# The head of a decoder trunk: where the first modulation sums are computed, and in which order its tiles are split

## The chip, the cores and the metric

One core of a Trainium2 chip runs the kernel. The metric is device microseconds of a whole execution. Three runs of the kernel before gave 1766.54, 1766.80 and 1773.45, median 1766.8. The profiled execution took 1766.12, its span is 1764.3.

## The reference

One layer on 2048 tokens of width 1024. The change lies in the first line's `shift` and `scale` and in the first projections.

```python
mod = jax.nn.silu(c) @ w_ada[l] + b_ada[l]
shift, scale, gate = jnp.split(mod, 3, axis=-1)
u = x * (1.0 + scale[:, None, :]) + shift[:, None, :]
h = u @ w_in[l]
q, k, v, a_gate, p_in, p_gate, m_a, m_p = jnp.split(h, offsets, axis=-1)
a = sliding_window_sink_attention(q, k, v, sinks[l], bias, mask) * jax.nn.silu(a_gate)
...
y = (y @ w_out[l]) * (1.0 + gate[:, None, :])
x = layer_norm(DEEPNORM_ALPHA * x + y, ln_gain[l], ln_bias[l])
```

## The kernel before

**Numbers.** A f32 value is held as a high part (a cast to a shorter f32 form, done on ACT) and a low part (value minus high part, done on DVE). A product of two such values is three TensorE products: high by high, high by low, low by high (`mm3`). I call these three a triple.

**Products.** The projections use a Strassen-like scheme with seven products instead of eight. A group of the work has two quads; a quad is two weight tiles of 128 columns of `w_in`, and each works on the sets named B11, T1, T2, B21, T3, B22 and T4. A set holds the high and low parts of one quarter of the transposed `u`, or of a sum or difference of quarters, in four tiles of 128 rows by 512 tokens. For each quad the weights are needed in three pairs (`first`, `second`, `third`) and one last half. A pair is split into parts by `pair_split`: a cast on ACT and a subtraction on DVE, each of 128x1024. `sum1`, `mid` and `late` make the sums of the weight quarters.

**The order.** PE, ACT, DVE, POOL and SP each run their own queue in order. Most operations of the head go through a helper that keeps program order, so all have one line in the profile, L56. In the rings after the head, work is hung on places of a group (a position counts ticks, one about every twelve products), and `steps` spreads a list of work over the places from a start on.

**The head** (`head`) opens the program. It computes shift and scale for the eight 128-row tiles k = 0 to 7, modulates the first half of the tokens, builds the sets and begins the first group.

- `load(k)`, on SP: two weight tiles of `w_ada` of 512 KB each, one for shift (`wadat`, laid out for TensorE) and one for scale (`wada`, laid out with the outputs on partitions), and 512 KB of `x`. After tiles 0 and 1 come the four weight quarters of a quad of the first group, 1 MB.
- `opening(k)`: `pe_modulation` multiplies the shift weights, as the stationary side, with single columns of silu(c), in 8 f32 products of 128x1. `modulation` computes scale on DVE as a product and sum over 1024 elements (CUSTOM_DVE_ANT_0 in the profile), and then adds PE's column to shift.
- `difference(k)` on DVE, for k below 4: the T1 difference before modulation. `modulate_x(k)` on ACT: both halves of the tile, in place.
- `middle(k)`: the parts of B11 (k below 4) or B21, one after the other; for k from 4 the raw T2 sum. `closing(k)`: the parts of T1 or T2, two tiles behind.
- `products(i)`: the triples of tile i for B11 and T1 and both quads, three tiles behind `opening`. `second_pair(x)` and `more` make the second pair of a quad and the triples of T2 and B21.
- `rest_sums(i)`: the sums for T3 and T4. Then the parts of T3, and in `first_phase` those of B22 and T4 at positions 4 and 6 of the first group. The same function spreads the second half's work (`sums_to`) from places 4, 29, 57 and 80 on.

The ring (`ring`, `back`) then adds the copies to the products (L380, L383), splits the third pair (L132 for its low part), and runs T3, B22 and T4 for each quad and B11 and T1 for the next group.

Of the kernel before, what the change touches and what calls it, by code (L numbers as in the profile page):

```python
# [12 lines left out]
F32 = mybir.dt.float32  # L13
# [6 lines left out]
P = 128  # L20
# [39 lines left out]
def kernel(  # L60
# [215 lines left out]
    class Quad:  # L276
# [7 lines left out]
        def load(self, ph, own, q=nc.sync, e=nc.gpsimd):  # L284
# [4 lines left out]
            q.dma_start(x[:, 0::3, :], by_two(self.srcs[0]))  # L289
# [824 lines left out]
    def head(ph):  # L1114
# [6 lines left out]
        early = [pl.tile([P, 4 * D], F32, tag=f"set_{n}", name=f"head_{n}") for n, pl in (("B22", cp), ("T3", ph.t), ("T4", ph.t))]  # L1121
        places = [t[:, i * D : (i + 1) * D] for t in (*early, big) for i in range(4)]
        ws = [places[2 * k : 2 * k + 2] for k in range(KT)]
        late = [small[:, i * D : (i + 1) * D] for i in range(2)]
# [15 lines left out]
        def load(k):  # L1140
            for w, m in zip(ws[k], (k, KT + k)):
                sp.dma_start(w, (wadat if m < KT else wada)[m])
# [12 lines left out]
        def pe_modulation(k):  # L1155
            sums[k] = bank(("pv", "pt", "lg", "lg")[k % 4])
            for i in range(KT):
                mm(sums[k][:, 0:1], ws[k][0][:, i * P : (i + 1) * P], ct[:, i : i + 1], start=i == 0, stop=i == KT - 1)

        def modulation(k):  # L1160
            m = KT + k
            w = ws[k][1]
            dve.tensor_tensor_reduce(w, w, cb, 1.0, mod[:, m : m + 1], ALU.mult, ALU.add, mod[:, m : m + 1])
            dve.tensor_tensor(mod[:, k : k + 1], mod[:, k : k + 1], sums[k][:, 0:1], ALU.add)
# [11 lines left out]
        def opening(k):  # L1176
            pe_modulation(k)
            modulation(k)

        def middle(k):  # L1180

            b1, b2 = xs[k]
            if k < 4:
                pool.dma_start(b12_d[k // 2, :, k % 2, :], b2)
            else:
                dve.scalar_tensor_tensor(ts[k - 4], ts[k - 4], sg[:, k - 4 : k - 3], b2, ALU.mult, ALU.add)
            parts("B11" if k < 4 else "B21", k % 4, b1)

# [5 lines left out]
        def closing(k):  # L1194
            if k >= 4:
                parts("T2", k - 4, ts[k - 4])
                return
            hi, lo = sets["T1"][:, k, 0, :], sets["T1"][:, k, 1, :]
            scale = mod[:, KT + k : KT + k + 1]
# [4 lines left out]
        def rest_sums(i):  # L1204
            minus(xs[i][0], ts[i], xs[i][0])
            minus(xs[4 + i][0], xs[4 + i][0], ts[i])
# [276 lines left out]
```

## Time and profile before

| what | value |
|---|---|
| median of 3 runs | 1766.8 us |
| profiled execution | 1766.12 us |
| its span | 1764.3 us |
| PE busy | 1702.9 us, 97% |
| DVE busy | 1206.0 us, 68% |
| ACT busy | 931.8 us, 53% |
| first 512-wide product on PE | 29.93 us |
| last product of T2 and B21 in the head | 64.8 us |

PE counts as busy whenever a product is under way, so its share says nothing on how fast it goes. A timeline row gives start, duration, engine, line, operation, output, input and count, then in brackets the idle time ahead of it and what ended it. Rows that follow each other closely overlap a little: the distance of two starts is the price, the duration has the pipeline's tail in it.

### The profile page before, as it was taken

The page shows a single profiled execution, that of the slowest core. Times are in us where ns is not written, and L with a number is a line of the kernel's source. Part 1 is how long each engine was busy: PE and PEld are TensorE (multiplying, and loading weights), DVE is VectorE, ACT ScalarE, POOL GpSimd, SP SyncE. Part 2 cuts the span into 40 slices and gives each one's busy share as a digit, 9 for nine tenths or more (in the row PEclk, how much of TensorE's full clock was granted, in tenths as well). Part 3 has the DMA queues.
Part 4 walks back from the last instruction along what each step waited for, and adds up shares of the span by engine and source line. Part 5 has one row for each costly group of instructions (what it writes and reads, how often), then busy time and mean ns, then how long its engine had stood idle before and what let it go on. Part 6 is the DMA issues. An engine that isn't in the chain of part 4 may idle for free. (4 is left out here: it accounts for less than half of the span.)

```text
span 1764.3 us, 24983 instructions
## 1 busy us (share of the span) xinstructions
PE 1702.9 (97%) x8248; PEld 1428.7 (81%) x8248; DVE 1206.0 (68%) x2180; ACT 931.8 (53%) x1969; POOL 792.7 (45%) x618
## 2 busy tenths in 40 slices
PE   6899999999999998999999999999999989999996
PEld 5688888888888887888788888888888768888785
DVE  5967665655777786766655367777867586765777
ACT  4544444545777775454444377777744333423451
POOL 2145454431356567434434125456762562364542
PEclk9999999999999999999999999999999999999998
DMA  9384767743354567687777634544796585689432
GB/s 365 112 279 179 270 210 273 271 148 132 108 173 146 172 219 294 245 281 254 246 274 262 231 98 132 175 155 149 258 356 225 182 257 182 226 314 384 166 143 99
DMA packets 180609, 381.30 MB, mean 216 GB/s; under 512 B 18800, under 2 KB 39296, under 8 KB 180480
## 3 DMA queue, kind: packets, MB, share of 16 engines
q1 hardware_dynamic: 173696, 363.66, 59.2%
q0 software_dynamic: 3552, 11.56, 1.7%
q10 hardware_dynamic: 3232, 4.49, 0.9%
q8 instruction: 65, 1.06, 0.2%
q14 instruction: 64, 0.52, 0.1%
HBM read 244.35 MB, written 138.44 MB: 217 GB/s over the span
## 5 line engine op out<-in xcount | busy, mean ns | idle before, releaser
L56 PE MATMUL mm<-set_B,w_set 128*128 128x512 f32 x3240 | 801.8, 396 | 17.5 <-DVE w_set L132 8.7
L56 PEld LDWEIGHTS mm<-set_B,w_set 128*128 128x128 f32 x3240 | 604.2, 189 | 147.4 <-DVE w_set L132 15.2
L56 PE MATMUL lg<-set_T,w_set 128*128 128x512 f32 x2088 | 505.9, 392 | 14.0 <-DVE w_set L132 8.6
L56 PEld LDWEIGHTS lg<-set_T,w_set 128*128 128x128 f32 x2088 | 390.8, 188 | 103.7 <-DVE w_set L132 14.0
L132 DVE TENSOR_TENSOR w_set<-W,w_set 128x1024 fp32r<-128x1024 f32 x162 | 224.1, 1383 | 175.7 <-ACT w_set L325 171.4
L325 ACT CAST w_set<-W 128x1024 fp32r<-128x1024 f32 x162 | 169.7, 1049 | 242.4 <-PE mm L56 195.6
L56 PE MATMUL mm<-set_T,w_set 128*128 128x512 f32 x1080 | 266.2, 394 | 0.0
L56 PEld LDWEIGHTS mm<-set_T,w_set 128*128 128x128 f32 x1080 | 201.1, 189 | 41.3
L294 POOL TENSOR_TENSOR W<-W,A 128x512 f32<-128x512 f32 x56 | 82.1, 1466 | 221.7 <-DMA W<-in_win_dram 55.9
L303 POOL TENSOR_TENSOR W<-W 128x512 f32<-128x512 f32 x56 | 80.1, 1431 | 155.5 <-DVE w_set L132 143.9
L56 DVE TENSOR_TENSOR o<-pv,o 64x128 f32<-64x128 f32 x256 | 72.4, 283 | 88.3 <-ACT o L56 85.4
L56 ACT ACTIVATE L<-L,nm 128x257 f32<-128x257 f32 (+1 forms) x256 | 127.2, 498 | 9.3 <-DVE nm L56 3.9
L298 POOL TENSOR_TENSOR W<-W 128x512 f32<-128x512 f32 x56 | 88.1, 1574 | 93.8 <-DVE w_set L132 84.7
L56 DVE CUSTOM_DVE_ANT_0 L<-lg,bt,nsink 128x256 f32<-128x256 f32 (+1 forms) x256 | 111.6, 473 | 5.0 <-PE lg L56 0.8
L299 POOL TENSOR_TENSOR W<-W 128x512 f32<-128x512 f32 x56 | 88.1, 1573 | 37.3 <-DMA W<-in_win_dram 28.1
L56 POOL TENSOR_TENSOR w_set<-W,w_set 128x1024 fp32r<-128x1024 f32 x14 | 33.7, 2405 | 139.6 <-ACT w_set L56 97.0
L56 POOL TENSOR_TENSOR p<-nxt,pg 128x512 f32<-128x512 f32 x32 | 42.0, 1311 | 106.4 <-DVE sm L56 102.8
L56 ACT COPY o<-pv 64x256 f32<-64x256 f32 x128 | 47.3, 370 | 78.1 <-PE pv L56 77.3
L56 DVE TENSOR_TENSOR ptl<-pt,pth 128x512 fp32r<-128x512 f32 (+1 forms) x128 | 85.7, 669 | 1.9 <-ACT pth L56 1.7
L56 DVE TENSOR_TENSOR k_lo<-spare,k_hi 128x512 fp32r<-128x512 f32 x61 | 63.2, 1041 | 28.8 <-ACT k_hi L56 15.0
L56 PE MATMUL lg<-kk,qs 128*128 128x256 f32 (+1 forms) x512 | 80.5, 279 | 0.0
L56 ACT ACTIVATE L<-L,sm 128x256 f32<-128x256 f32 (+1 forms) x128 | 64.3, 502 | 29.4 <-DVE sm L56 29.4
(208 smaller groups left out, 2304.9 us busy)
## 6 DMA issues: line engine op xcount, KB each, us to landing
W<-in_win_dram SPq DMA_DIRECT2D x48, 512.0 KB, 5.3
w_set<-wmix_d SPq DMA_DIRECT2D x32, 512.0 KB, 5.2
W<-in_win_dram SPq DMA_DIRECT2D x34, 256.0 KB, 3.4
A<-in_win_dram SPq DMA_DIRECT2D x34, 256.0 KB, 5.0
ag_d<-sig SPq DMA_DIRECT2D x32, 256.0 KB, 3.3
pg_d<-sig SPq DMA_DIRECT2D x32, 256.0 KB, 3.7
ma_d<-sig SPq DMA_DIRECT2D x32, 256.0 KB, 3.9
mp_d<-sig SPq DMA_DIRECT2D x32, 256.0 KB, 3.8
```

Of the source, the lines that this page charges most:

```text
L56: return lambda *args, **kw: self.tc.keep_in_program_order(op(*args, **kw))
L132: engine.tensor_tensor(dst, src, as32(hi), ALU.subtract)
L294: e.tensor_tensor(self.w[:, 1, :], self.w[:, 2, :], self.a22, ALU.add)
L298: e.tensor_tensor(x[:, 1, :], x[:, 1, :], x[:, 0, :], ALU.subtract)
L299: e.tensor_tensor(x[:, 2, :], x[:, 0, :], x[:, 2, :], ALU.subtract)
L303: e.tensor_tensor(x[:, 3, :], x[:, 3, :], x[:, 1, :], ALU.subtract)
L325: a.copy(by_two(hi), raw)
```

## The change

All of it is in the head, the load of a quad, and some places of the first ring.

- The modulation weights are the moving side: `pe_rows(k)` multiplies one column of silu(c) as the stationary side with 128 columns of weights, 8 f32 products for a row of 128 results on one partition. ACT copies the row to SBUF, and `pe_columns(k)` turns it to a column with a one-element product.
- For tiles 0 to 3 TensorE computes both rows, shift and scale. The scale weights of these tiles come in TensorE's layout, and DVE's sum over 1024 elements goes. For tiles 4 to 7 scale stays on DVE.
- `keep_going(n)` puts n products of the 128x128 identity with itself on PE: 18 ahead of the first row, 8 behind the first columns.
- `high(k)` makes the high parts of a tile on ACT, `rest_of(k)` the low parts on DVE one tile later. T2 is likewise cut into `raw_t2`, `high_t2` and `low_t2`. `difference(k)` stands ahead of the sum.
- The first pair of each quad is split one by one, behind tiles 0 and 1, instead of both behind tile 2. The products of tile k-2 stand one quad ahead of the row of tile k and one quad behind it. The second pairs stand in the turns k = 6 and 7.
- One weight quarter of each quad is loaded later, behind tiles 4 and 5.
- The sums for T3 stand at the end of the head, each ahead of its parts; those for T4 move to position 5 of the first ring, the late weight sum of the second quad to position 0, and the second half's work starts at 6 and 30 in place of 4 and 29.
- The tiles in which weights wait are taken in another order (T4, T3, B22).

```diff
-        def load(self, ph, own, q=nc.sync, e=nc.gpsimd):
+        def load(self, ph, own, q=nc.sync, e=nc.gpsimd, a12=True):
...
-            q.dma_start(x[:, 0::3, :], by_two(self.srcs[0]))
+            if a12:
+                q.dma_start(x[:, 0::3, :], by_two(self.srcs[0]))
+            else:
+                q.dma_start(x[:, 0, :], self.srcs[0][:, 0:CH])
...
-                sp.dma_start(w, (wadat if m < KT else wada)[m])
+                sp.dma_start(w, (wadat if m < KT or k < 4 else wada)[m])
...
-        def pe_modulation(k):
-            sums[k] = bank(("pv", "pt", "lg", "lg")[k % 4])
-            for i in range(KT):
-                mm(sums[k][:, 0:1], ws[k][0][:, i * P : (i + 1) * P], ct[:, i : i + 1], start=i == 0, stop=i == KT - 1)
+        def rows_of(k):
+            return 2 if k < 4 else 1
+
+        def pe_rows(k):
+            sums[k] = bank(("pv", "pt")[k % 2])
+            for r in range(rows_of(k)):
+                for i in range(KT):
+                    mm(
+                        sums[k][0:1, r * P : (r + 1) * P],
+                        ct[:, i : i + 1],
+                        ws[k][r][:, i * P : (i + 1) * P],
+                        start=i == 0,
+                        stop=i == KT - 1,
+                    )
+            n = rows_of(k) * P
+            act.copy(row_of(k)[:, 0:n], sums[k][0:1, 0:n])
+
+        def pe_columns(k):
+            for r in range(rows_of(k)):
+                mm(sums[k][:, 2 * P + r : 2 * P + r + 1], row_of(k)[:, r * P : (r + 1) * P], one, start=True, stop=True)
...
+        def high(k):
+            if k < 4:
+                pool.dma_start(b12_d[k // 2, :, k % 2, :], xs[k][1])
+            act.copy(part("B11" if k < 4 else "B21", k % 4, 0), xs[k][0])
+            if k < 4:
+                scale = mod[:, KT + k : KT + k + 1]
+                act.activation(part("T1", k, 0), ts[k], AF.Copy, scale=scale)
+                act.activation(sg[:, k : k + 1], scale, AF.Copy, scale=-1.0)
+
+        def rest_of(k):
+            name = "B11" if k < 4 else "B21"
+            low(dve, part(name, k % 4, 1), xs[k][0], part(name, k % 4, 0))
+            if k < 4:
+                scale = mod[:, KT + k : KT + k + 1]
+                dve.scalar_tensor_tensor(part("T1", k, 1), ts[k], scale, as32(part("T1", k, 0)), ALU.mult, ALU.subtract)
...
+        def keep_going(n):
+            acc = bank("lg")
+            for i in range(n):
+                mm(acc[:, 0:P], ident, ident, start=True, stop=True)
+
+        keep_going(18)
+        pe_rows(0)
+        pe_columns(0)
+        keep_going(8)
         difference(0)
+        modulation(0)
         modulate_x(0)
-        opening(1)
+        high(0)
+        first_pair(0)
+        pe_rows(1)
+        pe_columns(1)
         difference(1)
-        middle(0)
+        modulation(1)
         modulate_x(1)
+        rest_of(0)
+        high(1)
+        first_pair(1)
+        grp[0].mid(dve)
...
         for k in range(2, KT):
-            opening(k)
+            if k < 6:
+                products(k - 2, 0)
+            pe_rows(k)
+            if k < 6:
+                products(k - 2, 1)
+            if k == 7:
+                more(0, "B21", 0, 1)
+            pe_columns(k)
             if k < 4:
                 difference(k)
-            if k == 7:
-                second_pair(0)
-            closing(k - 2)
-            middle(k - 1)
-            if k == 2:
-                for q in grp:
-                    q.sum1(dve)
-                    starts.append(pair_split(ph, q.first(), act, dve))
-            modulate_x(k)
-            if k in (3, 4):
-                grp[k - 3].mid(dve)
-            if 3 <= k < 7:
-                products(k - 3)
-            if k > 5:
-                rest_sums(k - 6)
+            modulation(k)
+            modulate_x(k)
+            high(k)
+            if k > 4:
+                raw_t2(k - 1)
+                high_t2(k - 1)
+            rest_of(k - 1)
+            if k > 5:
+                low_t2(k - 2)
+                second_pair(k - 6)
+            if k == 2:
+                grp[1].mid(dve)
...
+        late_sets(ph.t, "T3")
+        for i in range(4):
+            t3_sum(i)
+            parts("T3", i, xs[i][0])
...
+        rest = (0, lambda: grp[1].late(dve)), (4, late_parts("B22", 1)), (5, t4_sums), (6, late_parts("T4", 0))
...
-            steps(hooks, groups, (4, 29, 57, 80)[i], todo)
+            steps(hooks, groups, (6, 30, 57, 80)[i], todo)
```

112 lines of the change are left out of this document (56 added, 56 removed).

## The prediction

> **What bounds the kernel now.** I read the page first: TensorE is busy 97% of the span, so only a stage where it waits or runs slowly can give time back. Cutting the span into stretches finds them; the columns of the first fence are the stretch, its length, and busy time (and count) of PE, PEld, DVE, ACT and POOL, then granted clock, DMA share and GB/s.
>
> ```profile
> core 0: us, PE busy (x) PEld busy (x) DVE busy (x) ACT busy (x) POOL busy (x), PEclk, DMA share, GB/s
> 30.00:65.00 35.00, 33.98 (x161) 28.08 (x160) 32.63 (x56) 23.46 (x39) 1.08 (x2) 0.95 0.44 172
> 65.00:92.00 27.00, 19.66 (x75) 15.14 (x76) 25.34 (x33) 16.58 (x28) 7.99 (x6) 0.94 0.63 220
> 110.00:200.00 90.00, 89.64 (x418) 74.25 (x417) 60.92 (x68) 39.06 (x59) 43.10 (x33) 1.00 0.65 224
> ```
>
> From 110 us on PE lacks 0.36 us in 90; nothing the change touches is left there. So all is decided before about 92 us. The timeline of PE, its time, duration, and idle time before it with what ended it:
>
> ```profile
> 7.79 3.55 PE L56 MATMUL pv<-ct,head_B 128*128 128x1 f32 x16 [7.79 <-DMA head_B<-in_wadat_dram]
> 14.76 3.57 PE L56 MATMUL pt<-ct,head_B 128*128 128x1 f32 x16 [3.43 <-DMA head_B<-in_wadat_dram]
> 21.32 3.57 PE L56 MATMUL lg<-ct,head_T 128*128 128x1 f32 x16 [2.99 <-DMA head_T<-in_wadat_dram]
> 26.50 3.57 PE L56 MATMUL lg<-ct,head_T 128*128 128x1 f32 x16 [1.61 <-DMA head_T<-in_wadat_dram]
> 29.93 1.63 PE L56 MATMUL mm<-set_B,w_set 128*128 128x512 f32 x3
> 32.64 1.48 PE L56 MATMUL mm<-set_B,w_set 128*128 128x512 f32 x3
> 39.34 0.84 PE L56 MATMUL mm<-set_T,w_set 128*128 128x512 f32 x3
> 40.02 1.84 PE L56 MATMUL pt<-ct,head_T 128*128 128x1 f32 x16
> 41.73 0.93 PE L56 MATMUL mm<-set_B,w_set 128*128 128x512 f32 x3
> 53.95 3.33 PE L56 MATMUL mm<-set_B,w_set 128*128 128x512 f32 x9
> 58.51 2.20 PE L56 MATMUL mm<-set_B,w_set 128*128 128x512 f32 x9
> 63.95 0.84 PE L56 MATMUL mm<-set_B,w_set 128*128 128x512 f32 x3
> 67.63 0.73 PE L56 MATMUL lg<-set_T,w_set 128*128 128x512 f32 x2 [2.84 <-DVE mm L383]
> 69.95 4.13 PE L56 MATMUL lg<-set_T,w_set 128*128 128x512 f32 x10 [1.59 <-DVE w_set L132]
> 73.92 2.90 PE L56 MATMUL mm<-set_B,w_set 128*128 128x512 f32 x12
> 84.18 5.31 PE L56 MATMUL lg<-set_T,w_set 128*128 128x512 f32 x22 [1.37 <-DVE w_set L132]
> 91.70 2.60 PE L56 MATMUL mm<-set_B,w_set 128*128 128x512 f32 x10 [1.75 <-DVE w_set L132]
> ```
>
> PE waits for DMA until 29.93, works without a break through the head's products to 64.8, then stands behind DVE three times until 91.70. A triple (three products of 512 columns) takes 1.48 us early and 0.84 later, 0.68 from start to start (39.34 to 40.02): the clock is at half until about 36 us, though the granted column of the page shows nothing of it. Half clock returns at 53.95 (nine products in 3.33 us against 2.20) and at 69.95.
>
> DVE and ACT give the prices of the chain that each tile's modulation runs through:
>
> ```profile
> 9.62 1.28 DVE L56 CUSTOM_DVE_ANT_0 head_B<-head_B,cb,mod 128x1024 f32<-128x1024 f32 x1 [0.86 <-DMA head_B<-in_wada_dram]
> 16.03 1.28 DVE L56 CUSTOM_DVE_ANT_0 head_B<-head_B,cb,mod 128x1024 f32<-128x1024 f32 x1 [3.87 <-DMA head_B<-in_wada_dram]
> 37.13 1.28 DVE L56 CUSTOM_DVE_ANT_0 head_T<-head_T,cb,mod 128x1024 f32<-128x1024 f32 x1
> 38.33 0.15 DVE L56 TENSOR_TENSOR mod<-mod,pv 128x1 f32<-128x1 f32 x1
> 38.40 0.75 DVE L56 SCALAR_TENSOR_TENSOR set_T<-head_B,mod,set_T 128x512 fp32r<-128x512 f32 x1
> 39.06 0.69 DVE L56 TENSOR_TENSOR set_B<-x,set_B 128x512 fp32r<-128x512 f32 x1
> 39.66 1.29 DVE L56 TENSOR_TENSOR W<-W 128x512 f32<-128x512 f32 x2
> 50.98 0.16 DVE L56 TENSOR_TENSOR mod<-mod,lg 128x1 f32<-128x1 f32 x1
> 51.06 1.22 DVE L56 TENSOR_TENSOR w_set<-W,w_set 128x1024 fp32r<-128x1024 f32 x1
> 64.53 0.70 DVE L380 TENSOR_TENSOR lg<-lg,u 128x512 f32<-128x512 f32 x1
> 82.78 1.95 DVE L132 TENSOR_TENSOR w_set<-A,w_set 128x512 fp32r<-128x512 f32 x2
> ```
>
> ```profile
> 38.52 0.82 ACT L56 ACTIVATE x<-x,mod 128x512 f32<-128x512 f32 x1 [1.00 <-DVE mod L56]
> 39.24 0.80 ACT L56 ACTIVATE A<-A,mod 128x512 f32<-128x512 f32 x1
> 39.95 0.71 ACT L56 ACTIVATE set_T<-head_B,mod 128x512 fp32r<-128x512 f32 x1
> 40.66 0.60 ACT L56 CAST set_B<-x 128x512 fp32r<-128x512 f32 x1
> 54.10 1.04 ACT L56 CAST w_set<-W 128x1024 fp32r<-128x1024 f32 x1
> 55.05 0.58 ACT L56 COPY u<-mm 128x512 f32<-128x512 f32 x1
> L56 ACT COPY o<-pv 64x256 f32<-64x256 f32 x128 | 47.3, 370 | 78.1 <-PE pv L56 77.3
> ```
>
> From start to start DVE takes 1.20 for a weight reduction, 0.66 for a scaled subtraction, 0.60 for a plain one of 512, 1.13 for one of 1024; ACT 0.71 per modulation, about 0.5 per cast of 512, 0.95 per cast of 1024.
>
> **The change, part by part.** *Moving weights.* A row now is 8 f32 products with one column of c as stationary side and 128 columns moving. No such instruction is in the trace. Each f32 product leaves two records (x16 for 8). Low bound: a record streams 128 columns at the pace of the 512-wide products (0.68/3/4 = 0.057 us), 16 x 0.057 = 0.91 us a row. High bound on the quick clock: today's row, 1.71 us (40.02 to 41.73); on the half clock 3.57. I take 1.71: the row there is also f32 in two records. The Trainium skill, "FP8 and Floating Point Precision" (TensorE Precision Notes), counts four passes through the array for true FP32; by that estimate a row would be 8 x 4 x 0.057 = 1.8 us, and the eight rows on the path 0.9 us dearer in all; no row of this case shows it.
>
> New after each row: an ACT copy of 256 or 128 elements on one partition (between nothing and the 0.58 of 512 columns; I take the nearest row, 64x256, 0.37) and two or one one-element products (two records of about 0.11 each, 0.44 or 0.22 in all). Against that DVE loses four reductions of 1.20, which in tiles 0 and 1 end before PE's result anyway. The difference now stands ahead of the sum, so ACT no longer waits 0.6 for it.
>
> *Identity products.*
>
> ```profile
> 1.01 0.29 POOL masks.py:199 TENSOR_SCALAR_AFFINE_SELECT ident<-ident 128x128 f32<-128x128 f32 x1
> ```
>
> POOL has the identity ready at 1.3 us, and 18 products follow; at today's half-clock pace of 0.44 each (3.55/8) they end at 9.3, with the clock released on the way at about 7.5. The second row of tile 0 lands at 9.62, as the reduction's input did, so they are hidden or nearly; 8 more fill 12.4 to 14.2. What they buy is the quick clock at the first products.
>
> *Loads.* Tiles 0 and 1 fetch 256 KB less each before the next tile, and hand it back after tiles 4 and 5. Between 14.76 and 21.32 five loads of 512 KB landed, 0.66 us per 256 KB: tile 1 lands 0.66 earlier, tiles 2 to 4 1.3 earlier, 6 and 7 where they were. SP issues two DMAs more, while it waits for landings in any case: nothing.
>
> *The walk.* Tile 0: row one 7.8 to 9.5, row two 9.6 to 11.4, copy to 11.9, column products to 12.4, shift and scale at 12.5. Tile 1: weights at 14.1 and 15.4, rows to 17.7, copy, columns at 18.65, sums at 18.8. First product 18.65, against 29.93. That is the gain: 11 us of head start, on the quick clock.
>
> From there each tile's shift and scale is a chain. The products of tile k-2 wait for DVE's low parts, which stand behind the sum of tile k-1; then the rows of k, then the second quad's products, then the columns, then DVE's sum. For k = 2 and 3: low-part wait 0.85, twice two triples 2.72, two rows 3.42, columns 0.44, sum and hand-overs 0.2: about 7.2 us. For k = 4 and 5 with one row: 5.3. So the sums stand at 26.0, 33.1, 38.4 and 43.6 (k = 5). The loads are earlier each time. Tile 6 has no products; its row's copy stands on ACT behind two modulations, a cast and the T2 cast of tile 4 (2.5 us), and the sum comes at 46.9. Tile 7's columns stand behind a product of the second pair: ACT needs 1.42 + 0.5 + 0.5 + 1.04 before that pair's high part, DVE 1.13 for the low part, then 1.2 for the reduction: 53.0, where the kernel before has 50.98. The head start is used up.
>
> The second quad's pair comes last: 53.1 + 1.42 + 0.5 + 0.5 + 1.04 = 56.6, low part at 57.8. PE stands 2.9 us and again 0.8 for it, and then has a third of a triple and 12 triples, 8.4 us: 66.2 on the quick clock. But PE did under 3 us of work in the nine before. At 53.95 the kernel before paid 1.1 us for such a stretch, at 69.95 1.86 (4.13 against 2.27): I add 1.5. End of the T2/B21 products 67.7, against 64.8.
>
> The Trainium skill, "TensorE: Matmul & The Clock Gate" (HAM oscillation — how this bites in real kernels), warns of idle gaps over about 3.4 us. The rows go further: at 53.95 no gap of that length stands ahead of the slow products, and by the rule alone the 1.5 us would not be added and the sum would be 1.5 lower.
>
> T3: DVE starts its adds when T2 of the first quad is complete (66.3) and has nine of 0.6 and one of 1.13 before the pair's low part, now with the third and fourth T3 parts and the late sum among them: 6.6 us where the kernel before took 5.4 (64.53 to 69.9). T3 goes on at 72.9, between 71.5 and 73.5, against 69.95: +1.5 to +3.5. B22's parts and late sum are then done, so nothing new waits there.
>
> The ten products behind that point took 4.13 us on the half clock; on the quick one 2.27. Which it will be depends on the clock's phase; I take the mean, 0.9 less than before.
>
> T4: its sums (4 x 0.6, moved here) and parts stand behind the second quad's T3. In the kernel before, T4 went on 10.2 us after T3's first quad (74.0 to 84.18); with the moved sums 10.2 to 12, I take 11.1. The fetch of the next rows moves from tick 4 to 6, so DVE's work for it no longer stands ahead of the next group's first pair, and the wait of 1.75 at 91.70 goes. Sum at that product: +2.9 (T3) - 0.9 (clock) + 0.9 (T4) - 1.75 = +1.2 us. On this execution's 1766.1 (span 1764.3 and 1.8 around it) that is 1767.3; the median of the runs shown, 1766.8, lies 0.7 above this execution. I forecast 1767.
>
> **The rivals.** *Rows at the low bound.* If a row costs 0.91, tiles 2 and 3 get 1.6 shorter each, 4 and 5 0.8: 4.8 in all, and later links follow. 1767 - 5 = 1762. For it: the 512-wide products move columns at that pace, and nothing in the trace excludes it here. Against it: the f32 row costs 1.71 today, on the side that is loaded.
>
> *The clock stays at half (the other side).* If moving rows with a one-column stationary side don't hold the clock up, the six rows of tiles 2 to 5 cost 3.57 (+1.86 each, 11 us) and their 16 triples up to 0.6 more each (9.6): between 1777 and 1787. It decides from a row of 2.9 us on. For it: 128x1 records ran ahead of the half clock at 53.95. Against: those moved one column, these 128.
>
> *The head start survives.* If the last pair isn't waited for, PE's head work from 18.65 (eight rows, 13.7; 32 triples, 21.8; columns, 1.8) ends at 56 instead of 66, T3 moves with it: 1757 at best. Against it: ACT's and DVE's queues of tiles 6 and 7, counted above.
>
> *Nothing moves*, since DVE bounds the stretch from 65 to 92 (25.34 of 27 us busy): 1766, the forecast's own range.
>
> **How the numbers follow.** A move of 0.5%, 8.8 us, is about what a measurement of this kernel can tell from none. Chances: forecast with "nothing moves" 0.60, 1763 to 1771; low-bound rows 0.20; half clock 0.12; surviving head start 0.08. Faster 0.07 (most of the last), slower 0.12, same 0.81. The range reaches from the surviving head start to the cheap end of the half clock, and leaves out what lies beyond both: 1757 to 1777.
>
> **What would show it.** Right: first 512-wide product near 18.7 and under 0.85 us a triple; rows of 16 records near 1.7; DVE idle before the sums of tiles 2 to 5; the sum of tile 7 near 53; PE idle near 54 to 57; T3 later than 69.95, no wait of 1.75 before the next group. Wrong: rows near 0.9 or 3.5, triples of 1.48 between 20 and 45, or products of the second pair without a wait.

## The result, and the profile after

The changed kernel takes 1782.89 us (median of six runs, 1776.18 to 1787.35), the kernel before 1768.89 beside it: 1.0075 times as long, 95% interval 1.0056 to 1.0095. It is 14 us slower; 1767 was forecast, the range ended at 1777. The profiled execution is the longest of the six (1787.35, span 1785.5), so it ends 21 us behind the one of before, where the medians differ by 14.

First the stretches, with the same columns as for the kernel before:

```profile
30.00:65.00 35.00, 29.15 (x154) 19.26 (x152) 19.27 (x35) 17.42 (x32) 0.54 (x1) 0.88 0.44 171
65.00:92.00 27.00, 22.01 (x80) 17.12 (x79) 22.06 (x33) 13.26 (x23) 3.91 (x3) 0.84 0.45 155
110.00:200.00 90.00, 88.40 (x406) 72.25 (x404) 59.37 (x67) 40.14 (x62) 39.28 (x30) 1.00 0.67 232
```

In the 35 us from 30 on PE was busy 33.98 before, now 29.15, at a granted clock of 0.88. The next 27 us hold more PE time, but at a clock of 0.84 and with hardly more products (80 records for 75). And from 110 us on, where PE lacked 0.36 us, it now lacks 1.60. Rows of the timeline of PE:

```profile
1.35 6.31 PE L56 MATMUL lg<-ident 128*128 128x128 f32 x36 [1.35 <-POOL ident masks.py:199]
7.93 3.65 PE L56 MATMUL pv<-head_T,ct 128*1 128x128 f32 x32 [0.27 <-DMA head_T<-in_wadat_dram]
18.65 0.60 PE L56 MATMUL pt<-ident,row 1*128 1x1 f32 x4 [0.45 <-ACT row L56]
19.18 0.50 PE L56 MATMUL mm<-set_B,w_set 128*128 128x512 f32 x1
20.17 0.72 PE L56 MATMUL mm<-set_B,w_set 128*128 128x512 f32 x2 [0.49 <-DVE set_B L56]
21.52 3.65 PE L56 MATMUL pv<-head_T,ct 128*1 128x128 f32 x32
25.11 0.96 PE L56 MATMUL mm<-set_B,w_set 128*128 128x512 f32 x3
25.91 0.86 PE L56 MATMUL mm<-set_T,w_set 128*128 128x512 f32 x3
26.70 0.60 PE L56 MATMUL pv<-ident,head_vv 1*128 1x1 f32 x4
27.23 0.50 PE L56 MATMUL mm<-set_B,w_set 128*128 128x512 f32 x1
...
37.64 1.91 PE L56 MATMUL pv<-head_B,ct 128*1 128x128 f32 x16
39.48 0.96 PE L56 MATMUL mm<-set_B,w_set 128*128 128x512 f32 x3
...
55.08 1.28 PE L56 MATMUL mm<-set_B,w_set 128*128 128x512 f32 x3 [2.42 <-ACT u L56]
60.65 2.05 PE L56 MATMUL lg<-set_T,w_set 128*128 128x512 f32 x3 [1.30 <-ACT w_set L56]
72.15 0.84 PE L56 MATMUL lg<-set_T,w_set 128*128 128x512 f32 x3
78.72 4.63 PE L56 MATMUL lg<-set_T,w_set 128*128 128x512 f32 x10 [2.98 <-DVE w_set L132]
83.15 3.37 PE L56 MATMUL mm<-set_B,w_set 128*128 128x512 f32 x12
96.62 6.91 PE L56 MATMUL lg<-set_T,w_set 128*128 128x512 f32 x22 [4.10 <-DVE w_set L132]
103.36 2.93 PE L56 MATMUL mm<-set_B,w_set 128*128 128x512 f32 x12
106.13 2.88 PE L56 MATMUL mm<-set_T,w_set 128*128 128x512 f32 x12
```

The head starts as forecast: the first product at 19.18 (29.93 before), on the quick clock. Then the head start melts: T2 and B21 end at 73.0 (64.8 before), T3 goes on at 78.72 (69.95), T4 at 96.62 (84.18), and the T1 products of the next group start at 106.13. In the timeline of PE of the kernel before they started 12 us earlier:

```profile
94.14 2.89 PE L56 MATMUL mm<-set_T,w_set 128*128 128x512 f32 x12
```

I call this distance the lag at the next group. DVE shows the sums of the modulation, and the orders on which T3 and T4 wait:

```profile
19.36 0.16 DVE L56 TENSOR_TENSOR mod<-mod,pt 128x2 f32<-128x2 f32 x1 [0.90 <-PE pt L56]
27.41 0.16 DVE L56 TENSOR_TENSOR mod<-mod,pv 128x2 f32<-128x2 f32 x1 [1.10 <-PE pv L56]
35.46 0.16 DVE L56 TENSOR_TENSOR mod<-mod,pt 128x2 f32<-128x2 f32 x1 [4.82 <-PE pt L56]
41.48 0.16 DVE L56 TENSOR_TENSOR mod<-mod,pv 128x1 f32<-128x1 f32 x1 [3.40 <-PE pv L56]
47.50 0.16 DVE L56 TENSOR_TENSOR mod<-mod,pt 128x1 f32<-128x1 f32 x1 [3.39 <-PE pt L56]
50.86 0.16 DVE L56 TENSOR_TENSOR mod<-mod,pv 128x1 f32<-128x1 f32 x1 [0.74 <-PE pv L56]
56.92 0.15 DVE L56 TENSOR_TENSOR mod<-mod,pt 128x1 f32<-128x1 f32 x1
75.56 0.69 DVE L56 TENSOR_TENSOR set_T<-x,set_T 128x512 fp32r<-128x512 f32 x1
77.45 1.22 DVE L132 TENSOR_TENSOR w_set<-W,w_set 128x1024 fp32r<-128x1024 f32 x1
85.99 1.78 DVE L56 TENSOR_TENSOR head_kk<-head_kk,head_T 128x512 f32<-128x512 f32 x1
91.30 3.46 DVE L56 TENSOR_TENSOR set_T<-head_vv,set_T 128x512 fp32r<-128x512 f32 x2
95.88 1.28 DVE L132 TENSOR_TENSOR w_set<-A,w_set 128x512 fp32r<-128x512 f32 x2
```

DVE now waits for PE before the sums of tiles 1 to 6; that of tile 7 follows DVE's own reduction without a wait and comes at 56.92 (50.98 before). Behind it the work is in series: the weight pair of T3 is split at 77.45, behind the last T3 part; T4's parts end at 94.7 and its weight's low part after that. Parts of T4 ran in slow rows in the kernel before, too:

```profile
77.06 1.79 DVE L56 TENSOR_TENSOR set_T<-head_kk,set_T 128x512 fp32r<-128x512 f32 x1
79.37 2.88 DVE L56 TENSOR_TENSOR set_T<-head_vv,set_T 128x512 fp32r<-128x512 f32 x2
```

The granted-clock records hold three stretches at half speed between 55 and 105 us: 10.2 us from 56.8, 6.8 from 77.3, 3.4 from 97.8 (before: 3.4 from 52.9 and 3.4 from 69.9).

### The profile page after: what moved, and what is told of

Read it like the earlier page. It is cut to its first block, busy times and chain, and to the rows that moved or that the text cites. A ratio compares the mean times of both kernels' runs of the same rounds, so it can differ in the third digit from the quotient of the medians.

```text
span 1785.5 us, 25283 instructions
## 1 busy us (share of the span) xinstructions
PE 1725.8 (97%) x8388; PEld 1437.4 (81%) x8388; DVE 1191.7 (67%) x2172; ACT 932.6 (52%) x1977; POOL 786.5 (44%) x618
## 4 chain that ended last, share of the span: by engine, by line
PE 76%; DMA 9%; DVE 6%; issue 3%; ACT 3%; POOL 3%; SPq 1%; POOLq 0%; DVEq 0%; ACTq 0%
PE mm L56 45%; PE lg L56 22%; PE pv L56 4%; PE pt L56 4%; DVE w_set L132 2%; DMA set_T<-ain_T_split 1%; DMA spare<-pin_T 1%; SPq L56 1%; POOL wide L574 1%; ACT w_set L328 1%; DMA spare<-ain_B 1%; DVE set_B L56 1%; DMA ma_d<-sig 1%; POOL a L56 0%; DVE set_T L56 0%
## 5 line engine op out<-in xcount | busy, mean ns | idle before, releaser
L56 PE MATMUL lg<-set_T,w_set 128*128 128x512 f32 x2088 | 512.6, 396 | 19.6 <-DVE w_set L132 13.2
L132 DVE TENSOR_TENSOR w_set<-W,w_set 128x1024 fp32r<-128x1024 f32 x162 | 223.3, 1379 | 181.7 <-ACT w_set L328 174.2
L56 ACT CAST pth<-pt 128x512 fp32r<-128x512 f32 (+1 forms) x128 | 73.5, 574 | 10.4
```

The source lines that it names most:

```text
L56: return lambda *args, **kw: self.tc.keep_in_program_order(op(*args, **kw))
L132: engine.tensor_tensor(dst, src, as32(hi), ALU.subtract)
```

## The experiments

Two theories at the start. A: the turns are series of waits, so the loss is made in the head, and T4's sums on DVE make it worse at T4. B: the clock, which falls to half in the late waits. In the table, "last sum" is tile 7's on DVE, "lag" the start of the next group's T1 products less 94.14, "time" the ratio's excess over 1 times 1767 us (its interval reaches 1.6 to 4.9 us to each side), and "behind" time less lag.

| run | edit | last sum | lag | median us | time | behind |
|---|---|---|---|---|---|---|
| changed | | 56.92 | 12.0 | 1782.89 | 13.3 | 1.3 |
| e1 | one row a tile | 54.92 | 4.1 | 1777.2 | 9.0 | 4.9 |
| e2 | rows ahead of the products | 56.80 | 10.9 | 1778.91 | 12.0 | 1.1 |
| e3 | T4's sums in the head | 57.04 | 8.0 | 1774.33 | 6.5 | -1.5 |
| e4 | places 4 and 29 | 57.85 | 13.6 | 1781.86 | 13.6 | 0.0 |
| e5 | products in the late waits | 56.86 | 10.4 | 1779.83 | 12.2 | 1.8 |
| e6 | no identity products | 58.71 | 13.0 | 1782.61 | 14.8 | 1.8 |
| e7 | before, with identity products | 51.61 | 0.6 | 1768.73 | 2.3 | 1.7 |
| e8 | e1, e3 and e5 | 55.30 | 3.2 | 1773.21 | 6.5 | 3.3 |
| e9 | low parts in their own turn | 55.56 | 5.4 | 1774.38 | 8.3 | 2.9 |
| e10 | second pair behind tile 7 | 54.52 | 8.5 | 1781.46 | 14.0 | 5.5 |
| e11 | e8, e9 and e10 | 54.40 | 1.8 | 1774.17 | 6.4 | 4.6 |
| e12 | before, places 6 and 30, late products | 51.12 | -3.8 | 1766.19 | -0.5 | 3.3 |
| e13 | T3's first weight pair early on DVE | 57.14 | 6.2 | 1778.32 | 9.9 | 3.7 |
| e14 | e11 with places 4 and 29 | 54.08 | 1.5 | 1768.67 | 1.2 | -0.3 |
| e15 | before, late products | 51.14 | 0.3 | 1767.5 | 0.7 | 0.4 |
| e16 | e3, e4 and e13 | 57.24 | 10.4 | 1776.25 | 8.1 | -2.3 |
| e17 | e14 and e13 | 54.16 | 3.4 | 1772.69 | 3.9 | 0.5 |
| e18 | before, places 6 and 30 | 49.41 | -3.5 | 1767.54 | 0.0 | 3.5 |

Marks come from one execution each: e18 leaves the head as it was, and its last sum came 1.6 us earlier. A lag is good to about that much. The half clock, too, falls elsewhere from run to run, and is part of what a lag shows.

The medians were taken beside different runs of the kernel before, so gains are safer read from the column "time". By it the changed kernel loses 13.3 us, with an interval of 9.9 to 16.8. The intervals of e3, e8, e11, e14 and e17 lie below this one, those of e1, e9, e13 and e16 overlap its lower end, and e2, e4, e5, e6 and e10 can't be told from the changed kernel.

**Rows (e1, e2).**

```diff
         def rows_of(k):
-            return 2 if k < 4 else 1
+            return 1
```

> The changed kernel with one row per tile on TensorE (scale of tiles 0 to 3 on DVE again, as before); all else as changed. Theory A (the head start is lost in the turns of tiles 2 to 7, where each sum waits on PE for rows, products and columns): tiles 2 and 3 lose a row of 1.8 us each, so the sum of tile 7 falls from 56.9 to 53.3 and the next group's first product follows by about 3 us; 1779 to 1780. Theory B (it is lost on DVE behind the head, by the work that was moved there): no better than the changed kernel, since DVE gets four reductions of 1.2 us back; 1783 to 1786.

The scale reductions of tiles 0 to 3 are back on DVE, and the row pairs on PE become single. The last sum comes 2.0 earlier, not 3.6: PE now waits 2.77 us at 20.23 for a low part (0.49 in the changed kernel), and the clock is at half from 20.3 to 23.7. The lag falls by 7.9, since T2 ends 4.4 earlier, behind 3.4 us of half clock and not 10.2, and T4's 22 products run on the quick clock (5.14 us and not 6.74). The median is 5.7 lower, the time 4.3: the second rows seem to cost more than they save, at the edge of the noise.

```diff
-            if k < 6:
-                products(k - 2, 0)
             pe_rows(k)
             if k < 6:
-                products(k - 2, 1)
+                products(k - 2, 0)
             if k == 7:
                 more(0, "B21", 0, 1)
             pe_columns(k)
+            if k < 6:
+                products(k - 2, 1)
```

> The changed kernel with the rows of tile k ahead of the first quad's products of tile k-2 and the columns ahead of the second quad's; same instructions. Theory A: the wait for the low part (0.5 us) and the second quad's two triples (1.6 us) leave the path from sum to sum, so turns 2 to 5 shorten from 8.0 and 6.0 to about 7.4 and 5.6 us (then PE itself is the bound), the sum of tile 7 comes 2 to 4 us earlier; 1779 to 1781. Theory B: the head moves, but T4 still starts near 96 and the total stays at 1783.

The sums of tiles 5 and 6 come at 46.34 and 50.46 in place of 47.50 and 50.86, the last one at 56.80: tile 7 waits for the second pair however early the others are. The median is 4 us lower, the time 1.3, which can't be told from nothing.

**T4's sums (e3).**

```diff
             t3_sum(i)
             parts("T3", i, xs[i][0])
+            minus(xs[4 + i][0], xs[4 + i][0], ts[i])
...
         def t4_sums():
-            for i in range(4):
-                minus(xs[4 + i][0], xs[4 + i][0], ts[i])
             late_sets(ph.t, "T4")
```

> The changed kernel with the four T4 sums back in the head, one behind each T3 tile, where DVE stands idle 2.8 us. Theory A: the wait of 4.1 us ahead of T4 shrinks by at most 1 us, as it comes from the lateness of T3 and from the two slow T4 parts; 1782 to 1783. Theory B: the 2.4 us of sums leave the queue ahead of T4, the wait shrinks by 2.4 to 3 us and the total by as much; 1779.5 to 1780.5.

PE of e3 at T3 and T4:

```profile
80.40 4.63 PE L56 MATMUL lg<-set_T,w_set 128*128 128x512 f32 x10 [3.04 <-DVE w_set L132]
93.90 5.67 PE L56 MATMUL lg<-set_T,w_set 128*128 128x512 f32 x24
```

T3 goes on 1.7 later, since four sums stand ahead of it, but T4 needs no wait and keeps the quick clock: 24 products in 5.67, where 22 took 6.91. 8.6 us off the median and 6.8 off the time, the largest single step.

**The places (e4).**

```diff
-            steps(hooks, groups, (6, 30, 57, 80)[i], todo)
+            steps(hooks, groups, (4, 29, 57, 80)[i], todo)
```

> The changed kernel with the second half's work at positions 4 and 29 of the first ring again in place of 6 and 30. Between 106 and 330 us the changed kernel's PE waits 4.9 us where the kernel before waits 1.1. If the two positions make these waits: PE waits about 1 us there and the total falls by 3 to 5 us, 1778 to 1780, less up to 1.8 us that come back as a wait ahead of the next group. If the waits come from the later start of the ring itself: no change there, 1783 or more.

1 us, within the interval. The lag rises by 1.6, and PE's waits between 110 and 335 us fall from 3.8 to 1.8: two effects that cancel here. e11, e14 and e18 take this up.

**The clock (e5, e6, e7).** e5 puts identity products into the late waits:

```diff
             if k == 7:
+                keep_going(8, "pv")
                 more(0, "B21", 0, 1)
...
         more(0, "B21", 1, 2)
+        keep_going(6, "pv")
         raw_t2(7)
...
         more(1, "T2", 3, 4)
+        keep_going(14, "pv")
         late_sets(ph.t, "T3")
```

> The changed kernel with identity products in the three late waits of PE: 8 behind the row of tile 7, 6 behind the first quad's second B21 triple, 14 behind the last T2 triple. Theory C (the half clock that follows those waits is a loss of its own): the half-clock stretch from 56.8 to 67.0 goes, the T2 and B21 products end near 69 in place of 73.0, T3's ten products take 2.3 us in place of 4.6; 1776 to 1779. Theory A or B alone: the clock rises and the waits for ACT and DVE grow by as much; 1782 to 1784.

```profile
77.86 2.58 PE L56 MATMUL lg<-set_T,w_set 128*128 128x512 f32 x10 [2.15 <-DVE w_set L132]
93.85 8.12 PE L56 MATMUL lg<-set_T,w_set 128*128 128x512 f32 x22 [4.66 <-DVE w_set L132]
```

T3's ten products fall from 4.63 to 2.58, yet PE then waits longer for DVE at T4, and falls to half there (8.12). The median falls by 3.1 us, the time by 1.1, which can't be told from nothing. Quick products at T3 alone bring little; e5 does not test a head without any half clock (3.4 us from 62.4 and 6.8 from 93.1 are left).

```diff
-        keep_going(18)
...
-        keep_going(8)
```

> The changed kernel without any identity products. If moving rows hold the clock up by themselves: the rows of tiles 0 and 1 run at half clock, the clock is full from about 18 us on, and the sum of tile 7 comes at most 2 us later; 1783 to 1785. If they don't: rows of 3.6 us each and triples of 1.48 past 25 us, sums later from tile to tile, as my rival of the half clock had it; 1788 to 1800.

The rows of tiles 0 and 1 without identity products:

```profile
7.83 6.33 PE L56 MATMUL pv<-head_T,ct 128*1 128x128 f32 x32 [7.83 <-DMA head_T<-in_wadat_dram]
15.20 3.65 PE L56 MATMUL pt<-head_T,ct 128*1 128x128 f32 x32
```

Tile 0 runs at half clock, tile 1 at full: two rows without a break raise the clock by themselves, and it stays full until 57.7. Rows don't hold it through every wait, though: in e1, e2, e8, e11 and e14 it is at half for 3.4 or 6.8 us between 18 and 32, beside PE waits of 1.58 to 2.78 us. The last sum is 1.8 later, the time the same. The identity products bring nothing that reaches the end.

```diff
+        keep_going(18)
         opening(0)
+        keep_going(12)
...
         opening(1)
+        keep_going(12)
...
+            if k == 2:
+                keep_going(8)
```

> The kernel before with identity products in PE's four first waits (18, 12, 12, 8) and nothing else. If the clock of the first products is worth something by itself: weight columns of tiles 1 to 3 take 1.7 us in place of 3.6, products run at 0.68 a triple from 28 us on, 1 to 4 us faster than the kernel before. If DVE bounds the head: PE waits longer for DVE and the time is that of the kernel before, within 1 us.

In the kernel before the same products do raise the clock, but it does not last. Its columns in tiles 0 and 1:

```profile
7.43 1.92 PE L56 MATMUL pv<-ct,head_B 128*128 128x1 f32 x16 [0.21 <-DMA head_B<-in_wadat_dram]
14.81 3.47 PE L56 MATMUL pt<-ct,head_B 128*128 128x1 f32 x16 [2.67 <-DMA head_B<-in_wadat_dram]
```

The clock, raised by then, is back at half in tile 1, behind a wait of 2.67 us. The last sum comes 0.6 later and the time is 0.2 to 4.4 us longer: that kernel gains nothing from a quick clock ahead of the first product either.

**Three together (e8).** The edits of e1, e3 and e5.

> One row per tile, T4 sums in the head and identity products in the late waits, together. If the three losses add: next group's first product near 91 (95.4 with one row, less the T4 wait of 2.8 and the slow T3 products), 1769 to 1772. If they overlap: no better than the T4 sums alone, 1774.

1773.21. Alone they gave 5.7, 8.6 and 3.1 of the median; together 9.7. By the time, e8 is no better than e3 alone (6.5 both): they shorten the same stretch, and do not add.

**Low parts (e9).**

```diff
-            rest_of(k - 1)
+            rest_of(k)
...
         high_t2(7)
-        rest_of(7)
```

(Tiles 0 and 1 likewise.)

> The changed kernel with the low parts' roundings and differences issued in their own tile's turn again, behind the casts (every rest_of one turn earlier). In the changed kernel PE waits some .5 us a turn at the low parts. Theory A (each turn is a series of sum wait, products, rows, columns, and what is late in it is added): the order on ACT and DVE changes, not the count, so the .5 a turn moves to the casts of the next tile or goes: the sums of tiles 2 to 5 come 0 to .5 earlier each, that of tile 7 at 55 to 57, and the time is 1780 to 1783. Rival, that the lag of the low parts carries the loss of the head: the sum of tile 7 comes at or under 53.0, and the time at 1776 or under. Second rival, that it is worth having: the sum of tile 7 past 58.5 and the time past 1785.

I expected 0 to 3 us and got 8.5 of the median (5.0 of the time). The median is the rival's, but its reason, a last sum under 53.0, is not: that came only 1.4 earlier. The gain is made later: T2 ends at 69.2 (73.0), with 3.4 us of half clock in place of 10.2, and T3 goes on at 72.20 (78.72). PE and DVE of e9 there:

```profile
72.20 4.60 PE L56 MATMUL lg<-set_T,w_set 128*128 128x512 f32 x12 [2.97 <-DVE mm L386]
```

```profile
69.11 1.22 DVE L132 TENSOR_TENSOR w_set<-W,w_set 128x1024 fp32r<-128x1024 f32 x1
72.65 0.68 DVE L56 TENSOR_TENSOR set_T<-x,set_T 128x512 fp32r<-128x512 f32 x1
```

The low part of T3's weights (L132) now runs ahead of the last T3 part, in the changed kernel behind it. The ring's splits are not in the helper that keeps program order; their place is decided when the program is built, and a small edit in the head moved it, though it names no line of the ring.

**That one place (e13).**

```diff
         for i in range(4):
+            if i == 2:
+                grp[0].w3 = pair_split(ph, grp[0].third(), act, dve)
             t3_sum(i)
...
-            w[x] = pair_split(ph, st[x][0].third())[::-1]
+            w[x] = (st[x][0].__dict__.pop("w3", None) or pair_split(ph, st[x][0].third()))[::-1]
```

> The changed kernel with the split of T3's first weight pair issued by name ahead of the third T3 sum, so that its low part stands before the last two T3 parts on DVE and not behind them. In the changed kernel this low part ran at 77.45 to 78.6, 5 us behind its cast, and T3's ten products waited 2.98 us for it. Order theory (e9's 8.5 us came mostly through this one place): T3 resumes at 74.5 to 76.5 instead of 78.72, T4 2 to 6 us earlier than 96.62, and the time is 1775 to 1779. Rival, that e9 gained by the clock alone (3.4 us at half instead of 10.2): the last sum and the end of T2 stay at 56.9 and 73, T3 gains under 1 us, and the time is 1781 to 1784.

```profile
76.05 2.34 PE L56 MATMUL lg<-set_T,w_set 128*128 128x512 f32 x9 [2.37 <-DVE mm L386]
89.03 3.49 PE L56 MATMUL lg<-set_T,w_set 128*128 128x512 f32 x14
```

T3 goes on 2.7 earlier, T4 begins without a wait, and 4.6 us of the median go (3.4 of the time) with the sums of the head unchanged. That is about half of e9's gain, as the order theory has it. It is not shown alone: this run also has no half clock at T3 and T4, only 6.8 us from 61.5, and its time is at the edge of the noise. The order, the half clock and the last sum are not parted in e9's gain.

**Tile 7 (e10).**

```diff
             modulation(k)
+            if k == 7:
+                second_pair(0)
             modulate_x(k)
...
-                second_pair(k - 6)
+                if k == 7:
+                    second_pair(1)
...
-            if k == 7:
-                more(0, "B21", 0, 1)
             pe_columns(k)
...
+        more(0, "B21", 0, 1)
         more(0, "T2", 0, 1)
```

> The changed kernel with the second pair's conversions and differences of its first tile issued behind modulation of tile 7, and the first pair's last product group behind the loop, so that nothing but the quads' products and the rows stands ahead of the last sum. Theory A: the sum of tile 7 comes at 53.5 to 55 instead of 56.92 (the 2 to 3 us that PE, ACT and DVE spend on the second pair ahead of it), but the products left over are run afterwards, while PE waits there anyway: T3 resumes 1 to 3 us earlier, and the time is 1779 to 1782. Rival, that the last T3 and T4 parts on DVE set the end, whatever the sums do: the next product group starts at the 103.36 of the changed kernel, and the time is 1782 to 1785.

The last sum comes at 54.52, as theory A says, and T3 goes on at 74.73, 4.0 earlier; the lag falls to 8.5. But the time is that of the changed kernel, so in the median of its runs the gain is lost behind the head. PE waits 6.7 us there between 100 and 400 us (5.9 in the changed kernel, 2.0 in the one before); this doesn't account for all of it.

**All, and the places again (e11, e14, e17).** e11 joins e1, e3, e5, e9 and e10 (tile 7's eight identity products stand behind its column here).

> The changed kernel with all that gained or might: one row a tile for scale, T4's sums back in the head, identity products in the late waits, low parts in their own turn, and the second pair of tile 7 behind its modulation. Theory A, that the loss is a sum of places: e1's -5.7 (1777.2), e3's -8.6 (1774.33) and e5's -3.1 (1779.83) share some, and e8 with the three of them gave 1773.21; two more of 0 to 3 us each give 1768 to 1773, and the next product group starts at 91 to 94.5. Rival, that a remainder of some 4 us lies behind the head, in the first ring: the next group is earlier than 94.5 and the time stays at 1772 to 1775.

The rival was right: the lag is 1.8, the time 6.4. DVE of e11 in the first ring:

```profile
102.21 0.69 DVE L56 TENSOR_TENSOR room_k<-spare,room_k 128x512 fp32r<-128x512 f32 x1 [3.42 <-DMA u_B_split<-room_k]
112.39 1.23 DVE L132 TENSOR_TENSOR w_set<-W,w_set 128x1024 fp32r<-128x1024 f32 x1 [2.84 <-ACT w_set L328]
```

The second half's work (room_k) stands 3.42 us for its stores, and PE waits seven times between 100 and 280 us, 4.3 us in all. e14 is e11 with the diff of e4:

> e11 with the second half's work at places 4 and 29 again. In e11 PE waited 4.3 us between 100 and 280 us in seven waits, against 1.12 in three in the kernel before. If the two places cause them: at most 2 us of waits there, a lag behind the kernel before at 380 us of 3 to 4.5 instead of 6.7, and 1770 to 1772.5. Rival, that the waits go with the load and weight order of the first groups, not with the places: 4 us of waits again and 1773 to 1775.

5.5 us lower, clear of the noise: behind this head the places cost that much. No loss that can be told is left: 1768.67, ratio 1.0007 (0.9996 to 1.0019) to the kernel before. So the six edits together cover the loss; which of them e14 needs is not known, and its identity products in the late waits are in neither kernel. e17 adds e13's diff to e14:

> e14 with T3's first weight pair split ahead of the third T3 sum. In e14 PE waits 3.49 us at 75.15 for the low part of that pair, and T3's ten products then take 4.15. If that wait shortens to 1 or less, T3 goes on at 71 to 73 and the next group starts at 89 to 91.5 instead of 92.91: 1765 to 1767.5. Rival, that DVE's work is only turned round, T4 and the next group come within 1 us of e14's, and the time is 1768 to 1769.5.

Slower than e14, 1772.69: T3 goes on at 70.7 without a wait, but PE then waits four times up to T4, 2.18 us the last time, and falls to half clock there. The work on DVE is only turned round, as the rival says, and what gained 4.6 us of the median in the changed kernel costs 4.0 here (by the time 3.4 and 2.7, both at the edge of the noise).

**The three moves behind the head (e16).** The diffs of e3, e4 and e13 together.

> The changed kernel with T4's sums back in the head, T3's first weight pair split ahead of the third T3 sum, and the second half's work at places 4 and 29. The turns of the head, its rows and identity products stay as changed, so the last sum stays at 56.9. If the three moves behind the head carry the loss (e3 -8.6 and e13 -4.6 on the changed kernel, the places -5.5 on e11): T3 resumes near 76, the next product group starts at 94 to 97, and the time is 1768 to 1771. If the late sum (56.9 against 50.98) has a share of its own that nothing behind it makes up: the next group at 97 to 100 and 1771 to 1775.

```profile
78.86 4.51 PE L56 MATMUL lg<-set_T,w_set 128*128 128x512 f32 x12 [5.04 <-DVE mm L386]
94.59 6.91 PE L56 MATMUL lg<-set_T,w_set 128*128 128x512 f32 x22 [2.49 <-DVE w_set L132]
```

1776.25, past both ranges, and T3 goes on at 78.86, not near 76. T4's sums and the weight split both stand ahead of DVE's sums into T3's banks now (L386), and PE waits 5.04 for these. Two moves that each bring T3 or T4 forward alone spoil each other. So whether the late sum of 57 has a share that no order could make up is not settled by it; e14, which comes out even, has its last sum at 54.08.

**The kernel before (e12, e15, e18).** e15 adds fourteen identity products behind its last T2 triple, e18 the places 6 and 30, e12 both.

```diff
+        keep_going(14, "pv")
         for i in (2, 3):
```

> The kernel before with fourteen identity products behind the last triple of T2 and nothing else: e12 without its two places. By the clock theory T3's ten products take 2.6 instead of 4.13, the wait of 1.75 ahead of the next group comes back as 1.5 to 4, since DVE's work for the second half stands there again. If e12's ring waits (0.52 at 100, 0.95 at 140) come from its places, they are gone here. Then the lag at 113 us is -1 to 0 and the time is 1765.5 to 1768; rival, that the gain at T3 passes through to the end: 1763 to 1765.

> The kernel before with the second half's work at places 6 and 30 instead of 4 and 29 and nothing else. The wait of 1.75 ahead of the next group is DVE's work at place 4: it goes or falls under 1. If the places cost only where DVE is already late, as behind the changed head: 1765 to 1768, the same as before. If they cost by themselves, as the 5.5 us between e11 and e14 could be read: over 1770.

> The kernel before with the two places of the steps that the change moves (6 and 30 for 4 and 29), and fourteen identity products behind the last triple of T2, where PE waits for T3's parts. In the kernel before, the ten products of T3 took 4.13 us at the half clock and one wait of 1.75 us stands ahead of the next product group at 91.70. If the half clock after late waits is a cost of its own (as e5's ten products at 2.58 instead of 4.63 say): the ten products take 2.3 to 2.7, the next group starts 2 to 4 us earlier, and the time is 1764 to 1767. Rival, that DVE's parts set T4 whatever PE's clock: T3's products are quick, PE waits longer for T4, the next group starts within 1 us of the kernel before, and the time is 1767 to 1770.

All three are the kernel before within the interval (0.9997 to 1.0004). e15 takes T3's ten products from 4.13 to 2.57, and the wait ahead of the next group grows from 1.75 to 2.79, with a half clock behind it. With places 6 and 30 that wait goes or shrinks (e18 none, e12 0.70): next group 3.5 and 3.8 earlier (1.6 of e18's come from its earlier head), and by about 197 us both have given back all but 0.5. No variant beats the kernel before by more than can be told.

Over the table: with places 6 and 30 a kernel loses 2.8 us on the mean behind the next group (13 kernels, -1.5 to 5.5), with 4 and 29 nothing (0.0 over the six, -2.3 to 1.7; the kernel before is the zero by definition). The later places trade a wait ahead of that group for waits in the ring; where no wait was left to save (e11), they only cost. In pairs only e11 and e14 show it clear of the noise; e4 beside the changed kernel and e18 beside the one before show no change of the time.

## Why the prediction was wrong

By its own steps, up to the T1 products of the next group, where it had +1.2 and 12.0 came: 10.8 us to explain.

- **Identity products, first product, no wait of 1.75:** right. The clock is full from 5.6 (7.5 forecast) and the eighteen end at 7.66 (9.3), the first product stands at 19.18 (18.65), the next group starts without the wait.
- **Price of a row, 1.71:** right; two take 3.59 (21.52 to 25.11), one 1.84 (37.64 to 39.48). The rival of 0.91 falls. The estimate of 1.8 from the Trainium skill, "FP8 and Floating Point Precision" (TensorE Precision Notes), four passes for true FP32, agrees with these rows.
- **The turns, "about 7.2 us" and 5.3: this step failed first.** They took 8.05 (19.36 to 27.41) and 6.02 (35.46 to 41.48). Nearly half of the error is a sum added wrongly: the terms as listed make 7.63 and, with the one-row column price of 0.22, 5.70; over four turns I used 24.8 where they give 26.7. The other 1.5 is size: the second quad's two triples took 1.59 between f32 products, not 1.36, the rows 0.17 a pair and 0.13 more, the columns 0.09 more each. With a first sum 0.6 late, the last one comes at 56.92 and not at 53.0: **3.9 us**. The steps of tiles 6 and 7, +3.3 and +6.1, were +3.36 and +6.06: right.
- **The half clock, "I add 1.5":** too small. T2 ends 16.1 behind the last sum, not 14.7 (**1.4**); T3's ten products took 4.43 from start to start and not 3.2 (**1.2**); T4's 22, 6.74 and not 5.15 (**1.6**). In this execution the half clock followed both late waits, T3's and T4's, where I had taken an even chance for T3 and none for T4; in e13 T3 runs quick behind a wait of 2.37. The row stands against the Trainium skill, "TensorE: Matmul & The Clock Gate" (HAM oscillation — how this bites in real kernels), as I read it: no gap of 3.4 us stands ahead of 56.8, where 10.2 us of half clock begin. But in e5 and e15 quick products at T3 are mostly eaten by the next wait for DVE.
- **T3, 5.2 behind T2's end:** 5.7 (**0.5**). The count was right: nine rows of 0.6 and the low part stand there, and take 6.9 (71.67 to 78.58) instead of 6.6. What I did not see is that the low part need not stand behind the last T3 part (e9, e13).
- **T4, 11.1 behind T3's first quad:** 13.5 (**2.4**). I priced the moved sums at 4 x 0.6 and took 0.9, as if over half of it fell into waits. They took 3.5 in full (85.39 to 88.90, one of them in a slow row of 1.78), and two more rows of L547 (1.2) and a wait for ACT (0.7) stand ahead of the weight's low part than before; a weight row of 1.14 less, and 1.2 less for T4's parts and low part, take some back. The slow rows of the parts (3.46 for two) explain nothing of the rise: the kernel before had them too (1.79 and 2.88). Undoing this move gives back 8.6 us of the median and 6.8 of the time (e3).
- These make 11.0; the first products of the next group gave 0.3 back (2.77 from start to start, 3.06 without the wait).
- **"From 110 us on ... nothing the change touches is left there":** wrong. In the profiled runs the lag grows from 12.0 to 18.3 by 381 us, by the medians 1.3 are left of that. A stretch in which PE lacks 0.36 us is full, but not safe: part of the new waits comes from the work hung on places 6 and 30 (3.8 us of waits between 110 and 335 us, 1.8 in e4).
- **The rivals:** the low-bound rows, the surviving head start and "nothing moves" are out. The slower rival had the side right and the reason wrong: the rows of the changed kernel ran on the full clock, up to 56.8; the half clock came after the waits that follow.

What no run parts: how the half clock and the order on DVE share the gains of e9 and e13, and what each of the six edits is worth within e14. The slow rows of DVE are taken up in the last section.

## What to carry to other kernels

An engine with little slack behind a stage (DVE from the last sum to T4) sets its end by the order of its queue, so list that order from the built program, operation by operation, for what was moved and for what stands behind it. Single edits to the changed kernel gave here 8.6, 8.5, 5.7, 4.6, 4.0 and 3.1 us of a median loss of 14 (6.8, 5.0, 4.3, 3.4, 1.3 and 1.1 by the time, of 13.3), more than the whole, because parts that wait for each other do not add and the smaller ones are within the noise; only joined edits show whether the loss is all found. And add up the listed terms once more before the sum is used.

## What was not expected of the hardware

- f32 rows of 128 moving columns on a one-column stationary side raise the clock from half to full: in e6 nothing else ran ahead of 13.3 us, where the clock rose, and the same 16 products took 6.33 us in tile 0 and 3.65 in tile 1. The columns of the kernel before stayed at half for four tiles (3.55 to 3.57 us each), but they are short and stand between waits of 1.6 to 3.4 us, so which of the two keeps the clock down is not told here.
- In the first 105 us of these runs the half clock came in stretches of 3.4, 6.8 and 10.2 us. The longest of the changed kernel began at 56.8, with no single gap of PE over 2.5 us in the ten before.
- Two triples between f32 rows and f32 columns took 0.80 and 0.79 us from start to start (25.11, 25.91, 26.70), against 0.68 among themselves (39.34 to 40.02 in the kernel before).
- DVE's slow rows stand only beside work of POOL. Between 60 and 400 us of the kernel before and the changed one, 34 single DVE rows of 128x512 took over 1 us, and each of them overlaps a row of POOL; of the 130 that POOL overlaps by 0.1 us at most, none did. Many rows beside POOL are quick, too. In the changed kernel the slow sum of 85.99 and the slow parts of 91.30 stand beside these:

```profile
85.49 1.74 POOL L302 TENSOR_TENSOR W<-W 128x512 f32<-128x512 f32 x1 [1.74 <-DMA W<-in_win_dram]
91.11 1.42 POOL L297 TENSOR_TENSOR W<-W,A 128x512 f32<-128x512 f32 x1 [3.89 <-DMA A<-in_win_dram]
92.61 1.60 POOL L302 TENSOR_TENSOR W<-W 128x512 f32<-128x512 f32 x1
```

In e13 it is POOL that is slow there (3.05 and 4.10 us for such rows at 85.54 and 88.68) and DVE's rows of 128x512 up to 91.6 are quick. So the two seem to hold each other up; no run takes POOL's work away to show it.
